# Stick-breaking heads: one summed tile for the last two key blocks

## The chip, the cores and the metric

The kernel runs on one core of a Trainium2 chip. The metric is the device time of one execution in microseconds. It is taken as the median of several runs; a profile is one further execution, recorded instruction by instruction. TensorE (PE in the profile) multiplies matrices into PSUM, VectorE (DVE) and ScalarE (ACT) do elementwise work, GpSimd (POOL) does a little masking and some transfers, and SyncE (SP) issues most transfers.

## The reference, cut to what matters

The program is one transformer block over 512 tokens of width 1024, in float32: a normalisation with modulation, a wide input projection, sixteen stick-breaking attention heads of width 64, four retention heads, a gated merge, and a feed-forward layer. The change touches only the stick-breaking heads:

```python
def stick_breaking_attention(q, k, v):
    s_len = q.shape[2]
    scale = SB_HEAD_DIM ** -0.5
    outs = []
    for i in range(s_len // BLOCK):
        end = (i + 1) * BLOCK
        qb = q[:, :, i * BLOCK:end]
        kb = k[:, :, :end]
        vb = v[:, :, :end]
        z = jnp.einsum('bhtd,bhsd->bhts', qb, kb).astype(jnp.float32) * scale
        ...
        log_1m_beta = jnp.where(mask, jax.nn.log_sigmoid(-z), 0.0)
        after = lax.cumsum(log_1m_beta, axis=3, reverse=True) - log_1m_beta
        log_a = jax.nn.log_sigmoid(z) + after
        a = jnp.where(mask, jnp.exp(log_a), 0.0)
        outs.append(jnp.einsum('bhts,bhsd->bhtd', a.astype(v.dtype), vb))
    return jnp.concatenate(outs, axis=2)
```

For each query the weight of a key is its own log-sigmoid plus the sum, over all later keys up to the query, of the log-sigmoid of the negated score, which is the negative of softplus(z). So a key's logarithm is z minus the sum of softplus over that key and every later one. With keys in blocks of 128, this sum has a part inside the key's own block, which a triangular matrix makes, and a part from all later blocks, for which a matrix of ones is enough.

## The kernel before, in words

**Layout.** Scores are held with keys on the 128 partitions and queries along the columns. Key block j (0 to 3) is needed by queries from j x 128 on, so block 0 has 512 columns, block 1 has 384, block 2 has 256 and block 3 has 128. The table `GEO` gives for each block its PSUM bank, its first column there, its first query and its width. Block 3 is held 256 wide, from query 256 on, with the mask over the part that it does not need, so that blocks 2 and 3 share one bank of 512 columns. There are three banks a head: bank 0 holds block 0, bank 1 holds block 1, bank 2 holds block 2 in its columns 0 to 255 and block 3 in its columns 256 to 511. Blocks 2 and 3 thus cover the same 256 queries.

**Precision.** TensorE takes its operands rounded, so a number that must keep float32 precision is split into a rounded part and the rest. `split` does that with a copy on ACT (the high part) and a subtraction on DVE (the low part). A product with an exact matrix, such as one of ones, takes two matmuls, one with each part. A product of two split operands takes three (`mm3`).

**One head, `sb_head(h)`.** It takes three banks from the pool of `z` and runs in four stages. First the scores of blocks 3, 2, 1, 0 are multiplied into the banks. Then, for the banks 2, 1, 0 in turn, softplus is computed: a mask with a minimum (line 607, DVE), the negated absolute value by an integer operation (609, DVE), exponential and logarithm (612 and 613, ACT), the sum with max(z, 0) (614, DVE) into a temporary `t`, and its split (616) into a pair from the pool `s`, kept as `sp[bank]`. In the third stage the suffix sums are subtracted from the scores in PSUM, bank after bank: block j gets `negtri` times its own softplus and `negones` times that of each later block; line 622 makes that list of terms and line 626 issues two matmuls for each. When a bank is complete, ACT takes its exponential (630) and it is split again (632). Fourth, the values are multiplied into a single bank `av` (640), ACT copies it out (642), a transfer exchanges the two halves of the partitions (644) and DVE adds them (645) into `o_sb`.

So for the third stage block 3 has one term, block 2 has two, block 1 three and block 0 four.

**Order.** Above the heads, the program is written as a sequence: for two pairs of heads at a time, the query and key projections (`sb_qk`, two products of 24 matmuls each) and some of the sixteen gates (`mix`, 24 matmuls each), then four heads, and so on; after the last heads come the last six gates, the splits of the results, and the output product `ps`. The order on each engine is not the written one. A planner at build time keeps, for each instruction, its place in the sequence as its priority, plays the program through with its own estimates of durations, and gives an engine the earliest written instruction that is ready. Matmuls of a projection or a gate, which are written later, therefore fill holes in which a head's next matmul isn't ready. On the chip each engine works through its queue in the order fixed by the planner and stands when the next instruction isn't ready.

**Buffers.** The temporaries `t` have seven slots for tiles of 128x512, the pairs `s` have eight, the banks `z` three, the banks `ps` four, `av` one; weights pass through three `raw`, four `whi` and four `wlo` tiles. SyncE's queue issues its transfers in one order, so an exchange at line 644 that waits holds the weight loads (line 202) behind it.

Of the kernel before, what the change touches and what calls it, by code (L numbers as in the profile page):

```python
# [12 lines left out]
F32R = mybir.dt.float32r  # L13
# [6 lines left out]
P = 128  # L20
D = 1024
S = 512
# [71 lines left out]
BUFS = dict(raw=3, araw=2, whi=4, wlo=4, h=8, q=8, v=4, s=8, qp=2, o=8, t=7, ps=4, z=3, av=1, sm=12)  # L94
# [16 lines left out]
GEO = ((0, 0, 0, 512), (1, 0, 128, 384), (2, 0, 256, 256), (2, 256, 256, 256))  # L111
# [4 lines left out]
def kernel(  # L116
# [9 lines left out]
    nc = tc.nc  # L126
# [3 lines left out]
    apool = ctx.enter_context(tc.tile_pool(name="apool", bufs=1))  # L130
# [5 lines left out]
    def nm(s):  # L136
        uid[0] += 1
        return f"{s}_{uid[0]}"
# [4 lines left out]
    def psa():  # L143
        return pspool.tile([P, S], F32, tag="av", bufs=BUFS["av"], name=nm("av"))

    def psz():
        return pspool.tile([P, S], F32, tag="z", bufs=BUFS["z"], name=nm("z"))

    def pair(tag):
        return apool.tile([P, 2, S], F32R, tag=tag, bufs=BUFS[tag], name=nm(tag))  # L150

    def tmp():
        return apool.tile([P, S], F32, tag="t", bufs=BUFS["t"], name=nm("t"))
# [7 lines left out]
    def f(ap):  # L161
        return ap.bitcast(F32)
# [32 lines left out]
    negtri = cpool.tile([P, P], F32R, name="negtri")  # L195
    negones = cpool.tile([P, P], F32R, name="negones")
# [8 lines left out]
    def split(dst_hi, dst_lo, src, scale=1.0, eng=None):  # L205

        nc.scalar.activation(dst_hi, src, AF.Copy, scale=scale)  # L207
        if isinstance(scale, float) and scale == 1.0:
            return (eng or nc.vector).tensor_sub(dst_lo, src, f(dst_hi))  # L209
        return nc.vector.scalar_tensor_tensor(  # L210
            dst_lo, src, scale, f(dst_hi), op0=ALU.mult, op1=ALU.subtract
        )
# [15 lines left out]
    def mm(o, lhs, rhs, start, stop):  # L228
        return nc.tensor.matmul(o, lhs, rhs, start=start, stop=stop, skip_group_check=True).ins  # L229
# [208 lines left out]
    with tc.manual_schedule(engines={nc.vector.engine, nc.scalar.engine, nc.tensor.engine}):  # L438

        nc.scalar.preload_act_table_set("natural_log_exp_and_others")  # L440
        c = sm[:, SM_C : SM_C + KT]
# [68 lines left out]
        for kt in range(KT):  # L510
# [12 lines left out]
            z = kt == KT - 1  # L523
# [70 lines left out]
    def sb_head(h):  # L594
        q, k, vt = sbq[h], sbk[h], sbv[h // 4]
        z = [psz(), psz(), psz()]
        for j in (3, 2, 1, 0):
            bank, c, t0, w = GEO[j]
            for i in range(2):
                head_pe[h] = mm(z[bank][:, c : c + w], k[:, j * P : (j + 1) * P], q[:, i, t0:S],  # L600
                                i == 0 and j != 2, i == 1)
        sp = {}
        for bank in (2, 1, 0):
            w = BANKW[bank]
            zb = z[bank][:, :w]
            m = S if bank == 2 else P
            nc.vector.tensor_tensor(zb[:, :m], zb[:, :m], maskc[:, :m], op=ALU.min)
            t = tmp()[:, :w]
            nc.vector.tensor_scalar(
                t.bitcast(I32), zb.bitcast(I32), -(2**31), None, op0=ALU.bitwise_or  # L610
            )
            nc.scalar.activation(t, t, AF.Exp)
            nc.scalar.activation(t, t, AF.Ln, bias=1.0)
            nc.vector.scalar_tensor_tensor(t, zb, 0.0, t, op0=ALU.max, op1=ALU.add)
            hl = pair("s")
            split(hl[:, 0, :w], hl[:, 1, :w], t)
            sp[bank] = hl
        avs = {}
        for bank in (2, 1, 0):
            for j in (3, 2) if bank == 2 else (bank,):  # L620
                _, c, t0, w = GEO[j]
                terms = [(negtri, j, t0)] + [(negones, jj, GEO[jj][2]) for jj in range(j + 1, 4)]
                for lhs, jj, tt in terms:
                    bj, cj, tj, wj = GEO[jj]
                    for i in range(2):
                        mm(z[bank][:, c + tt - t0 : c + w], lhs, sp[bj][:, i, cj : cj + wj],
                           False, False)
            w = BANKW[bank]
            t = tmp()[:, :w]
            nc.scalar.activation(t, z[bank][:, :w], AF.Exp)  # L630
            hl = pair("s")
            split(hl[:, 0, :w], hl[:, 1, :w], t)
            avs[bank] = hl
        o = psa()
        r, hf = (h % 4) // 2, h % 2
        for j in (3, 2, 1, 0):
            bank, c, t0, w = GEO[j]
            v = vt[j // 2][:, j % 2, r * 256 + hf * P : r * 256 + hf * P + P]
            for i in range(2):
                mm(o[:, t0:S], v, avs[bank][:, i, c : c + w], j == 3 and i == 0, j == 0 and i == 1)  # L640
        u, u2 = tmp(), tmp()
        nc.scalar.activation(u, o, AF.Copy)
        own, oth = (slice(0, HD), slice(HD, P)) if hf == 0 else (slice(HD, P), slice(0, HD))
        nc.sync.dma_start(u2[own], u[oth])
        nc.vector.tensor_add(o_sb[h // 2][own], u[own], u2[own])
# [3 lines left out]
    def sb_pair(p):  # L649
        o_sb[p] = otile()  # L650
        sb_head(2 * p)
        sb_head(2 * p + 1)
# [445 lines left out]
    for g, n in enumerate((2, 2, 4, 6)):  # L1098
        if g > 1:
            sb_v(g)  # L1100
        for p in (2 * g, 2 * g + 1):
            o_sb[p] = otile()
            for h in (2 * p, 2 * p + 1):
                with tc.issue_after(act_table.ins):
                    sb_head(h)
        if g < 3:
            sb_qk(2 * g + 2)
            mix(n // 2)
            sb_qk(2 * g + 3)
            mix(n - n // 2)  # L1110
        else:
            mix(n)
# [6 lines left out]
    for d in range(8):  # L1119
        o = ps()  # L1120
        gemm(o, weight(("ps", d)), acts)
        r, t = tmp(), tmp()
# [248 lines left out]
    for d in range(4):  # L1371
# [9 lines left out]
        with tc.issue_after(last_sq.ins), tc.issue_after(res.ins):  # L1381
# [3 lines left out]
            elif d == 1:  # L1385
                prepare(0, 2, "qq")
                t0 = sums_of[0]
# [340 lines left out]
```

## Time and profile before

| | |
|---|---|
| median of 3 runs | 1173.94 us (1172.72 to 1175.59) |
| span of the profiled execution | 1173.1 us |
| granted TensorE clock, mean | 0.998 |
| first mask of a head (line 607) | 492.6 us |
| first mask of the last bank of the last head | 714.0 us |
| HBM traffic over the span | 141 GB/s |

The profile's span is one execution's time from its first to its last instruction. A view that groups instructions names them by line, engine, operation and tile (`z<-s,negones` writes a `z` bank from an `s` tile and `negones`), then gives the count, the busy time and the mean of one in ns. Most matmuls stand at line 229, the helper that issues them, so they are told apart by tiles and shapes. A row of the timeline gives the start, the length and the merged count of like instructions that follow each other. Matmuls overlap, so the length of one is more than the distance from its start to the next one's. PEld is the load of the stationary operand.

### The profile page before, as it was taken

To read this page: it belongs to the slowest core of one execution; us is meant where nothing else is said; L and a number is where in the kernel's file an instruction comes from. 1 tells how busy PE (TensorE), PEld (TensorE's weight loads), DVE (VectorE), ACT (ScalarE), POOL (GpSimd) and SP (SyncE) were. 2 spreads that over 40 slices of the span, in tenths; PEclk is the share of its full clock that TensorE was granted. 3 is DMA by queue.
4 is the path that set the end of the run, shared out by engine and by line. 5 is a ranking of instruction groups with operands and counts; after the bars stand their busy time and mean duration, and the time that the engine had idled before them with its cause. 6 is when DMAs were issued, how large, how long until landed. Compare 5 with 4: busy or idle time off the path is not lost.

```text
span 1173.1 us, 16899 instructions
## 1 busy us (share of the span) xinstructions
PE 1156.8 (99%) x6476; PEld 1010.9 (86%) x6476; DVE 873.2 (74%) x1342; ACT 611.9 (52%) x928; POOL 50.1 (4%) x84
## 2 busy tenths in 40 slices
PE   8999999999999999999999999999999999999996
PEld 7898888888878888888888888879999999999996
DVE  7979966775764867478888688775998776777556
ACT  5444543343333444478778688354954444454433
POOL 0000000020002010000000000000100000000000
PEclk9999999999999999999999999999999999999999
DMA  9723536493566565846565545873545663565232
GB/s 358 256 68 113 185 103 208 154 260 115 161 201 176 181 159 185 232 123 180 153 173 133 153 126 179 283 235 103 113 136 179 184 161 116 148 186 152 86 89 72
DMA packets 64017, 192.88 MB, mean 164 GB/s; under 512 B 7744, under 2 KB 9920, under 8 KB 63936
## 3 DMA queue, kind: packets, MB, share of 16 engines
q1 hardware_dynamic: 56624, 172.92, 46.3%
q0 software_dynamic: 6768, 18.35, 8.8%
q8 instruction: 51, 0.84, 0.3%
q10 hardware_dynamic: 544, 0.52, 0.1%
q14 instruction: 30, 0.25, 0.1%
HBM read 146.15 MB, written 18.87 MB: 141 GB/s over the span
## 4 chain that ended last, share of the span: by engine, by line
PE 89%; DVE 4%; DMA 3%; ACT 2%; issue 1%; SPq 0%; DVEq 0%; ACTq 0%
PE ps L229 65%; PE z L229 21%; PE av L229 3%; DMA raw<-wp 2%; DMA araw<-wada 1%; DVE sraw L387 1%; ACT whi L207 1%; DVE wlo L209 1%; DMA o<-xT 0%; ACT s L207 0%; DVE wlo L418 0%; DVE t L425 0%; DVE araw L257 0%; DMA gspill<-g 0%; DVE t L476 0%
## 5 line engine op out<-in xcount | busy, mean ns | idle before, releaser
L229 PE MATMUL ps<-h,whi 128*128 128x512 f32 (+1 forms) x1410 | 416.9, 377 | 1.6 <-DVE h L209 0.8
L229 PEld LDWEIGHTS ps<-h,whi 128*128 128x128 f32 x1410 | 256.2, 188 | 47.7 <-ACT h L431 1.8
L229 PE MATMUL ps<-h,wlo 128*128 128x512 f32 (+1 forms) x705 | 262.1, 376 | 0.0
L207 ACT ACTIVATE whi<-raw 128x1024 fp32r<-128x1024 f32 (+1 forms) x122 | 127.4, 1044 | 192.3 <-PE ps L229 144.8
L209 DVE TENSOR_TENSOR wlo<-raw,whi 128x1024 fp32r<-128x1024 f32 (+1 forms) x122 | 146.6, 1204 | 61.9 <-ACT whi L207 60.8
L229 PEld LDWEIGHTS ps<-h,wlo 128*128 128x128 f32 x705 | 132.8, 188 | 23.2
L229 PE MATMUL ps<-s,whi 128*128 128x512 f32 x480 | 148.5, 390 | 0.7 <-DVE v L209 0.6
L229 PE MATMUL z<-q,whi 128*128 128x256 f32 x504 | 106.8, 283 | 0.0
L229 PEld LDWEIGHTS ps<-s,whi 128*128 128x128 f32 x480 | 89.2, 188 | 19.3 <-DVE v L209 1.0
L229 PE MATMUL ps<-s,wlo 128*128 128x512 f32 x240 | 93.4, 389 | 0.0
L207 ACT ACTIVATE s<-t 128x512 fp32r<-128x512 f32 (+1 forms) x134 | 74.4, 586 | 34.8 <-DVE t L789 21.4
L209 DVE TENSOR_TENSOR s<-t,s 128x512 fp32r<-128x512 f32 (+1 forms) x134 | 81.3, 637 | 9.6 <-ACT s L207 9.3
L229 PEld LDWEIGHTS z<-q,whi 128*128 128x128 f32 x504 | 84.9, 192 | 1.5
L1166 DVE SCALAR_TENSOR_TENSOR o<-ps,mod,o 128x512 f32<-128x512 f32 (+1 forms) x63 | 42.4, 680 | 32.6 <-PE ps L229 32.6
L229 PEld LDWEIGHTS ps<-s,wlo 128*128 128x128 f32 x240 | 45.1, 188 | 9.5
L877 ACT ACTIVATE whi<-s 128x1024 fp32r<-128x1024 f32 x33 | 34.9, 1056 | 33.6 <-PE ps L229 19.0
L229 PE MATMUL ps<-whi,h 128*128 128x512 f32 (+1 forms) x192 | 52.4, 354 | 0.0
L881 DVE TENSOR_TENSOR wlo<-s,whi 128x1024 fp32r<-128x1024 f32 x32 | 39.1, 1222 | 16.3 <-ACT whi L877 15.9
L229 PE MATMUL ps<-q,whi 128*128 128x256 f32 (+1 forms) x224 | 49.3, 313 | 0.0
L229 PE MATMUL z<-qp,whi 128*128 128x256 f32 x168 | 47.2, 283 | 0.0
L229 PE MATMUL z<-q,wlo 128*128 128x256 f32 x168 | 46.4, 283 | 0.0
L257 DVE SCALAR_TENSOR_TENSOR araw<-araw,cact 128x1024 f32<-128x1024 f32 x32 | 38.4, 1221 | 10.0 <-DMA araw<-wada 9.8
(311 smaller groups left out, 2063.1 us busy)
## 6 DMA issues: line engine op xcount, KB each, us to landing
raw<-wp SPq DMA_DIRECT2D x151, 512.0 KB, 4.0
araw<-wada SPq DMA_DIRECT2D x32, 512.0 KB, 4.5
araw<-wp SPq DMA_DIRECT2D x26, 512.0 KB, 4.6
sraw<-wada SPq DMA_DIRECT2D x16, 512.0 KB, 7.8
q<-qp SPq DMA_DIRECT2D x32, 256.0 KB, 3.7
s<-wp SPq DMA_DIRECT2D x12, 512.0 KB, 5.2
spill<-o POOLq DMA_DIRECT2D x24, 256.0 KB, 7.2
o<-xT SPq DMA_DIRECT2D x16, 256.0 KB, 3.7
```

Of the source, the lines that this page charges most:

```text
L207: nc.scalar.activation(dst_hi, src, AF.Copy, scale=scale)
L209: return (eng or nc.vector).tensor_sub(dst_lo, src, f(dst_hi))
L229: return nc.tensor.matmul(o, lhs, rhs, start=start, stop=stop, skip_group_check=True).ins
L257: nc.vector.scalar_tensor_tensor(raw, raw, 1.0, cact, op0=ALU.mult, op1=ALU.mult, accum_out=col)
L387: nc.vector.scalar_tensor_tensor(raw, raw, 1.0, cact, op0=ALU.mult, op1=ALU.mult, accum_out=col)
L877: nc.scalar.activation(hi, t, AF.Copy)
L881: nc.vector.tensor_sub(lo, t, f(hi))
L1166: return nc.vector.scalar_tensor_tensor(x1[d][:, hv], o[:, hv], mod[:, gcol + d : gcol + d + 1], x1[d][:, hv], op0=ALU.mult, op1=ALU.add,)
```

## The change

After the softplus of all three banks, the softplus of blocks 2 and 3, which lie side by side in bank 2's temporary and cover the same 256 queries, is added in place, and the sum is split into a tile `late` from the pool `t` (one tile holds both parts, 256 columns each). Blocks 1 and 0 then multiply `negones` with `late` once where they multiplied it with block 2 and with block 3. Block 0 keeps its separate term for block 1, and block 2 its term for block 3.

```diff
--- before.py
+++ after.py
@@ -615,16 +615,25 @@
             hl = pair("s")
             split(hl[:, 0, :w], hl[:, 1, :w], t)
             sp[bank] = hl
+            if bank == 2:
+                t2 = t
+        late = apool.tile([P, S], F32R, tag="t", bufs=BUFS["t"], name=nm("late")).rearrange("p (a b) -> p a b", a=2)
+        nc.vector.tensor_add(t2[:, 0:256], t2[:, 0:256], t2[:, 256:512])
+        split(late[:, 0, 0:256], late[:, 1, 0:256], t2[:, 0:256])
         avs = {}
         for bank in (2, 1, 0):
             for j in (3, 2) if bank == 2 else (bank,):
                 _, c, t0, w = GEO[j]
-                terms = [(negtri, j, t0)] + [(negones, jj, GEO[jj][2]) for jj in range(j + 1, 4)]
-                for lhs, jj, tt in terms:
-                    bj, cj, tj, wj = GEO[jj]
+                terms = [(negtri, t0, sp[bank][:, :, c : c + w])]
+                if j == 2:
+                    terms.append((negones, 256, sp[2][:, :, 256:512]))
+                elif j < 2:
+                    if j == 0:
+                        terms.append((negones, P, sp[1][:, :, 0:384]))
+                    terms.append((negones, 256, late[:, :, 0:256]))
+                for lhs, tt, x in terms:
                     for i in range(2):
-                        mm(z[bank][:, c + tt - t0 : c + w], lhs, sp[bj][:, i, cj : cj + wj],
-                           False, False)
+                        mm(z[bank][:, c + tt - t0 : c + w], lhs, x[:, i, :], False, False)
             w = BANKW[bank]
             t = tmp()[:, :w]
             nc.scalar.activation(t, z[bank][:, :w], AF.Exp)
```

## The prediction

> **What bounds the kernel now.** I read the page's busy table first, then the chain of waits by engine, then busy time by stretches around the stage that is edited.
>
> ```profile
> span 1173.1 us, 16899 instructions
> ...
> PE 1156.8 (99%) x6476; PEld 1010.9 (86%) x6476; DVE 873.2 (74%) x1342; ACT 611.9 (52%) x928; POOL 50.1 (4%) x84
> ...
> PE 89%; DVE 4%; DMA 3%; ACT 2%; issue 1%; SPq 0%; DVEq 0%; ACTq 0%
> ```
>
> ```profile
> 490.00:550.00 60.00, 59.95 (x308) 50.27 (x307) 47.55 (x81) 46.14 (x83) 0.00 (x0) 1.00 0.58 153
> 550.00:610.00 60.00, 60.00 (x306) 49.80 (x305) 49.74 (x84) 45.99 (x86) 0.00 (x0) 1.00 0.59 167
> 610.00:670.00 60.00, 60.00 (x305) 50.20 (x304) 47.88 (x77) 45.72 (x84) 0.00 (x0) 1.00 0.54 145
> 670.00:730.00 60.00, 60.00 (x309) 50.77 (x308) 49.55 (x82) 52.66 (x97) 0.00 (x0) 1.00 0.47 147
> 730.00:790.00 60.00, 58.81 (x258) 48.16 (x257) 43.81 (x60) 25.36 (x31) 1.73 (x2) 1.00 0.80 260
> ```
>
> The columns of the second fence are the stretch, then busy us of PE, PEld, DVE, ACT and POOL, the granted clock, the DMA share and GB/s. The sixteen heads run from 492 to 731 us, and there TensorE is never idle, at full clock. The heads alone could not do that: the projections of later pairs and the gates fill the holes of the heads' dependency chain.
>
> ```profile
> L229 PE MATMUL ps<-h,whi 128*128 128x512 f32 x422 | 135.5, 391 | 0.0
> ...
> L229 PE MATMUL z<-s,negones 128*128 128x256 f32 x160 | 26.8, 281 | 0.0
> ...
> L229 PE MATMUL z<-s,negones 128*128 128x384 f32 x32 | 8.3, 340 | 0.0
> ```
>
> These are groups of 490 to 730 us: group, count, busy us, mean ns of one. The first is the fill; with one `wlo` matmul to two `whi`, it is 633 matmuls. So the stage is a **queue of matmuls with fill to spare**: what leaves TensorE there leaves the time, as long as nothing new makes TensorE stand.
>
> The waits it has now, in the same stretch (who waited for whom: us, times, longest):
>
> ```profile
> PEld av L229 <- DVE s L209: 2.8, 10, 0.3
> PEld z L229 <- ACT s L207: 2.7, 11, 0.4
> PEld z L229 <- ACT t L630: 2.4, 9, 0.4
> ```
>
> That is 7.9 us in 30 waits, 0.26 us each and no longer than 0.4, for sixteen heads. A hand-off from DVE or ACT to TensorE is thus mostly covered by fill, and where it is not it costs a quarter of a microsecond.
>
> **Removed.** Per head the `negones` matmuls are twelve: two for block 2, four of 256 columns for block 1, and two of 384 and four of 256 for block 0 (192 in all, the 160 and 32 above). After the change blocks 1 and 0 take one product pair with the summed tile where they took two, so four matmuls of 128x256 go per head, **64 in all**. Their price is the distance between starts, since their ends overlap:
>
> ```profile
> 600.85 0.64 PE L229 MATMUL z<-s,negones 128*128 128x256 f32 x4
> ...
> 718.56 0.62 PE L229 MATMUL ps<-h,whi 128*128 128x512 f32 x2
> ```
>
> Four of 256 columns take 0.64 us, the last one 0.28 (its mean above), so a step is (0.64 - 0.28) / 3 = 0.120 us. For 512 columns it is 0.62 - 0.39 = 0.23, about twice that, so a step goes with the columns and not with the weight load. 64 x 0.120 = **7.7 us**. The other end is the busy share of the group, 26.8 / 160 = 0.168 us, which has some tails of lone matmuls in it: 10.7 us. I take 7.7, since these stand in runs.
>
> The Trainium skill, TensorE: Matmul & The Clock Gate, section on the back-to-back issue gap, gives N/2.4 + 2.5 ns for the gap of a lone matmul, 109 ns for 256 columns; by that the 64 would be an estimated 7.0 us. The trace has 120 ns, so the sum goes by that.
>
> **Added.** Per head an add of 128x256 on DVE, a copy of 128x256 on ACT and a subtraction of 128x256 on DVE. No DMA is added and none moves past another. The same forms stand elsewhere in this trace:
>
> ```profile
> L1407 DVE TENSOR_TENSOR t<-t,t 128x256 f32<-128x256 f32 x16 | 6.8, 422 | 3.9 <-ACT t L1403 2.7 <-ACT t L1576 1.2
> L207 ACT ACTIVATE s<-t 128x256 fp32r<-128x256 f32 x8 | 2.8, 404 | 0.4 <-DVE t L1040 0.4
> L209 DVE TENSOR_TENSOR s<-t,s 128x256 fp32r<-128x256 f32 x8 | 2.9, 418 | 0.0
> ```
>
> So 0.84 us of DVE and 0.40 us of ACT a head, 13.4 and 6.5 us in all. DVE was busy for 194.7 of the 240 us (the four rows added), ACT for 190.5; they go to 208 and 197 of about 235. Both still have room, so as work they cost nothing. The room is what hides them: without it, the two rows that grow would be a bound themselves.
>
> **Moved: the wait.** This is the term that can go either way. Block 1 could run when its own and bank 2's parts were split; now its last pair waits for the sum, whose three steps are issued behind all three banks. One head, in time:
>
> ```profile
> 607.56 1.74 DVE L609 TENSOR_SCALAR t<-z 128x512 int32<-128x512 int32 x3
> ...
> 612.03 0.68 DVE L209 TENSOR_TENSOR s<-t,s 128x512 fp32r<-128x512 f32 x1
> ...
> 612.63 0.68 DVE L614 SCALAR_TENSOR_TENSOR t<-z,t 128x512 f32<-128x512 f32 x1
> ...
> 614.30 1.22 DVE L209 TENSOR_TENSOR wlo<-raw,whi 128x1024 fp32r<-128x1024 f32 x1
> ...
> 614.75 0.64 PE L229 MATMUL z<-s,negones 128*128 128x256 f32 x4
> ...
> 615.42 0.49 ACT L630 ACTIVATE t<-z 128x384 f32<-128x384 f32 x1 [0.59 <-PE z L229]
> 615.43 0.68 DVE L209 TENSOR_TENSOR s<-t,s 128x512 fp32r<-128x512 f32 x1
> ...
> 616.47 1.16 DVE L209 TENSOR_TENSOR s<-t,s 128x512 fp32r<-128x512 f32 x2 [0.35 <-ACT s L207]
> ...
> 617.09 1.00 PE L229 MATMUL z<-s,negones 128*128 128x384 f32 x6
> ...
> 618.12 0.60 ACT L630 ACTIVATE t<-z 128x512 f32<-128x512 f32 x1 [1.28 <-PE z L229]
> ...
> 620.41 1.75 DVE L609 TENSOR_SCALAR t<-z 128x512 int32<-128x512 int32 x3
> ```
>
> Bank 2 is split at 612.7 and bank 0 at 616.1. If the three steps follow that, the sum is there at 616.1 + 0.42 + 0.40 + 0.42 = 617.3; if the two subtractions of 616.47 stand ahead of the last step, at 617.6 + 0.42 = 618.0. Two pairs of 0.24 us then end at 617.8 to 618.5. Block 1's exponential so starts some 2 to 3 us later than its 615.4, but block 0's, which ends the head, at most 0.4 us later than its 618.1, and its own 0.6 us behind block 1's 0.5 on ACT makes that up to 0.9. Behind the waiting weight load on TensorE's queue stand fill matmuls, and for their banks the gates on DVE and ACT wait. But the order is the planner's: a term that it expects late is put behind fill, as it does with bank 0 today (its six wait from 615.4 to 617.1 while TensorE is busy). I charge one extra wait of 0.26 us in every second head, 8 x 0.26 = **2.1 us**; the ends are 0 and all three steps bare, 16 x 1.24 = 19.9 us.
>
> What is late next: the next head's banks 1 and 0 and the exchange of halves behind the head, which holds the load queue:
>
> ```profile
> SPq L644 <- ACT t L642: 42.4, 15, 6.0
> ```
>
> It already stands 42.4 us for `u` in 490 to 800 us, 2.8 a time, without TensorE standing; 0.9 more a head at most is a third of that, and I charge nothing for it; it would come back as loads that are as much later, 16 x 0.9 = 14.4 us at the worst, inside the end already named. And heads are not back to back; the mask of a head's last bank and of the next head's first, across the last change of group, start at
>
> ```profile
> 646.04 0.30 DVE L607 TENSOR_TENSOR z<-z,table 128x128 f32<-128x128 f32 x1
> ...
> 672.22 0.89 DVE L607 TENSOR_TENSOR z<-z,table 128x512 f32<-128x512 f32 x2
> ```
>
> 26 us there, against the 12.8 from one head's `L609` to the next in the sequence above: some 13 us of slack before head 12, which is more than 11 x 0.9 = 9.9.
>
> **Buffers.** Nine `t` tiles a head where there were eight, on seven slots, and bank 2's is held until the add. I cost this at nothing: the sum is last read by bank 0's terms, at about 618.5, before the next head takes its three at 620.4. Without those 1.9 us the next head would start as much later as the sum, at most the 1.24 above. In return bank 2's `s` tile is free after block 2.
>
> **Sum.** -7.7 + 2.1 = -5.6. From the span, 1173.1 - 5.6 = 1167.5; the median of the runs, 1173.94, lies 0.8 above this execution's span, which I keep: **1168.3 us**. The stretch behind the heads loses TensorE 1.2 of 60 us to loads (fifth row of the stretches); its loads start as tiles of the heads' stage come free, so it moves along.
>
> **Rivals.**
>
> The heads' chain takes the place of the queue in the last four heads, behind which no further head waits as fill:
>
> ```profile
> 731.59 0.62 PE L229 MATMUL ps<-q,whi 128*128 128x512 f32 x2
> ...
> 731.98 0.69 DVE L209 TENSOR_TENSOR s<-o,s 128x512 fp32r<-128x512 f32 x1 [0.70 <-ACT s L207]
> ...
> 732.72 0.39 PE L229 MATMUL ps<-s,whi 128*128 128x512 f32 x1
> ```
>
> The first output product meets the last head's result just in time. If each of the four is late by the whole 1.24, 5.0 us are given back: 1168.3 + 5.0 = **1173.3**. Against it: at 731.59 the second product is already under way as fill, and its 21 matmuls that don't need that head are 4.8 us.
>
> TensorE has room that its busy share hides: weight loads are 86% of the span, so 14% of the steps might be idle and the removed matmuls come out of that. Then **1173.9**, unchanged. Against it: a load takes 188 ns
>
> ```profile
> L229 PEld LDWEIGHTS ps<-h,whi 128*128 128x128 f32 x1410 | 256.2, 188 | 47.7 <-ACT h L431 1.8
> ```
>
> and the steps of 0.120 us are shorter than that, so loads overlap, while the step doubles with the columns. The Trainium skill, Perfetto Trace Analysis, section on identifying the most-contended engine, says that matmul busy time is a poor measure and weight-load busy a better one; the starts in this trace speak for the columns as the limit.
>
> **Slower:** TensorE stands at the first product with the sum, in each head, because in the run DVE reaches the two added steps later than the planner thought (a `wlo` subtraction of 1.22 us is put in front, as at 614.30). It decides from 7.7 / 16 = 0.48 us of standing a head. With the three steps bare: 1173.9 - 7.7 + 19.9 = **1186.1**. For it: DVE goes from 81% to 88%. Against it: no wait of a weight load is over 0.4 us today.
>
> That the change does not do what it says I leave out: the loop of terms fixes the count.
>
> **How the numbers follow.** Forecast 0.62; the last four heads 0.16; room on TensorE 0.05; slower 0.17. A difference under 0.3%, 3.5 us, can't be told from none. Faster is thus 0.62, the same 0.21, slower 0.17. The forecast's own range is 1163.2 (10.7 removed, no wait) to 1170.4. The range of 8 in 10 runs from 1163 to 1178: it takes in the cases of no change and the near part of the slower one, and leaves out the bare steps.
>
> **What would show it.** 64 `z<-s,negones` matmuls and 64 with the new tile instead of 192; 32 new DVE and 16 new ACT instructions of 0.42 and 0.40 us; TensorE still at 60 of 60 in the four stretches, with the last head's `L645` some 5 us earlier; waits of weight loads for the new tile of about 2 us in total. It is wrong if those waits exceed 4 us, if TensorE shows idle time between 490 and 730 us, or if the heads end earlier but the span does not follow.

## The result and the profile after

| | before | changed |
|---|---|---|
| median of 4 runs each, same chip | 1173.55 us (1172.72 to 1175.59) | 1165.28 us (1164.15 to 1166.38) |
| ratio, 95% interval | | 0.9928 [0.9914, 0.9942] |
| span of the profiled execution | 1173.1 us | 1164.4 us |

The changed kernel is 8.3 us faster, 0.7%; the forecast was 5.6 us, and the time lies in its range. From line 628 on, lines of the changed kernel are 9 higher than before.

The page of the changed kernel, span, busy time and chain of waits:

```profile
span 1164.4 us, 16817 instructions
...
PE 1149.4 (99%) x6412; PEld 1003.9 (86%) x6412; DVE 882.9 (76%) x1374; ACT 616.8 (53%) x944; POOL 50.0 (4%) x84
...
PE 90%; DVE 4%; DMA 3%; ACT 2%; issue 1%; SPq 0%; DVEq 0%; ACTq 0%
```

There are 64 matmuls fewer, 32 DVE and 16 ACT instructions more. PE's busy time fell by 7.4 us and the span by 8.7. The groups of the changed kernel between 490 and 730 us (busy us, mean ns, idle before):

```profile
L229 PE MATMUL z<-late,negones 128*128 128x256 f32 x64 | 15.3, 289 | 0.0
...
L209 DVE TENSOR_TENSOR late<-t,late 128x256 fp32r<-128x256 f32 x16 | 6.7, 417 | 0.2 <-ACT late L207 0.2
L621 DVE TENSOR_TENSOR t<-t 128x256 f32<-128x256 f32 x16 | 6.6, 415 | 0.0
L207 ACT ACTIVATE late<-t 128x256 fp32r<-128x256 f32 x16 | 6.5, 407 | 0.6 <-DVE t L621 0.5
L229 PE MATMUL z<-s,negones 128*128 128x256 f32 x32 | 6.4, 282 | 0.0
```

With the 32 of 384 columns this is 64 and 64, as the forecast had it, at nearly the durations that it took from other stages (422 and 418 ns on DVE, 404 on ACT). The stretches of the changed kernel (busy us of PE, PEld, DVE, ACT and POOL, granted clock, DMA share, GB/s):

```profile
490.00:550.00 60.00, 60.00 (x303) 50.26 (x302) 52.44 (x92) 47.21 (x87) 0.00 (x0) 1.00 0.62 168
550.00:610.00 60.00, 60.00 (x300) 50.08 (x299) 51.32 (x91) 46.99 (x87) 0.00 (x0) 1.00 0.62 169
610.00:670.00 60.00, 60.00 (x301) 50.37 (x300) 53.59 (x93) 52.27 (x99) 0.00 (x0) 1.00 0.56 148
670.00:730.00 60.00, 59.71 (x295) 48.92 (x294) 49.60 (x84) 50.34 (x93) 0.00 (x0) 1.00 0.51 163
730.00:790.00 60.00, 59.51 (x282) 49.72 (x281) 47.72 (x64) 28.84 (x34) 2.58 (x3) 1.00 0.83 263
```

TensorE is still full while the heads run, but for 0.29 us in the fourth stretch. Its longest groups of waits there, 485 to 728 us, and the one for the new tile (us, times, longest):

```profile
PEld z L229 <- ACT s L207: 3.3, 15, 0.4
PEld av L229 <- ACT s L207: 1.6, 7, 0.4
...
PEld z L229 <- ACT late L207: 0.9, 3, 0.4
```

So the new wait is met three times in sixteen heads. One head of the changed kernel in time shows why:

```profile
615.54 0.61 ACT L207 ACTIVATE s<-t 128x512 fp32r<-128x512 f32 x1
615.71 0.41 DVE L621 TENSOR_TENSOR t<-t 128x256 f32<-128x256 f32 x1
...
616.16 0.42 ACT L207 ACTIVATE late<-t 128x256 fp32r<-128x256 f32 x1
...
616.64 0.68 DVE L209 TENSOR_TENSOR s<-t,s 128x512 fp32r<-128x512 f32 x1
...
617.24 0.41 DVE L209 TENSOR_TENSOR late<-t,late 128x256 fp32r<-128x256 f32 x1
...
617.48 0.28 PE L229 MATMUL z<-late,negones 128*128 128x256 f32 x1
...
618.65 0.40 PE L229 MATMUL z<-late,negones 128*128 128x256 f32 x2
618.68 1.01 ACT L639 ACTIVATE t<-z 128x384 f32<-128x384 f32 x2 [0.95 <-PE z L229]
```

The add at 615.71 runs while ACT copies bank 0, and slips in ahead of bank 0's own low part at 616.64. The sum is complete at 617.65, some 0.3 us behind that low part (617.32), and its last use is at 618.65. That is the common case: by the ends in the trace it is 0.3 us in ten of the sixteen heads, and over 2 us in three. Over the sixteen heads, from the first `L609` of a head to the end of its exponentials, block 1's comes 1.5 us later than before (10.78 us, before 9.27) and block 0's, which ends the head, 0.1 us (11.66, before 11.55); these four are means worked out from the starts and ends of the trace.

Where the gain appears is less plain. The last head's exchange is added (`o`) and the last gate (`g`) is made, in the kernel before, at the last time of each row (count, durations in ns, first to last start):

```profile
L645 DVE TENSOR_TENSOR o<-t,t x16: 673/686/692, 512.2 to 730.6; 64x512 f32<-64x512 f32 x16
```

```profile
L827 DVE TENSOR_SCALAR g<-ps,sm x16: 740/750/751, 475.6 to 727.0; 128x512 f32<-128x512 f32 x16
```

and in the changed kernel:

```profile
L654 DVE TENSOR_TENSOR o<-t,t x16: 671/686/690, 511.6 to 727.7; 64x512 f32<-64x512 f32 x16
```

```profile
L836 DVE TENSOR_SCALAR g<-ps,sm x16: 741/750/751, 475.8 to 717.6; 128x512 f32<-128x512 f32 x16
```

The heads end only 2.9 us earlier, the last gate 9.4 us earlier. The matmuls that were freed let the fill run ahead, while a head has become a little longer: 17.8 us from its first `L609` to its `o`, where it was 17.3 (means of sixteen). The rest of the gain is had behind the heads, where less fill is left over: from the last head's row to the end of the span it is 442.5 us before (1173.1 - 730.6) and 436.7 after (1164.4 - 727.7). The distance from the last gate to the last head grew from 3.6 to 10.1 us; it matters in the experiments.

### The profile page after: what moved, and what is told of

Its sections match the earlier page's. It is cut to its first block, busy times and chain, and to the rows that moved or that the text cites. A ratio compares the mean times of both kernels' runs of the same rounds, so it can differ in the third digit from the quotient of the medians.

```text
span 1164.4 us, 16817 instructions
## 1 busy us (share of the span) xinstructions
PE 1149.4 (99%) x6412; PEld 1003.9 (86%) x6412; DVE 882.9 (76%) x1374; ACT 616.8 (53%) x944; POOL 50.0 (4%) x84
## 4 chain that ended last, share of the span: by engine, by line
PE 90%; DVE 4%; DMA 3%; ACT 2%; issue 1%; SPq 0%; DVEq 0%; ACTq 0%
PE ps L229 66%; PE z L229 21%; PE av L229 3%; DMA raw<-wp 2%; DVE sraw L387 1%; DVE wlo L209 1%; ACT whi L207 1%; DMA t<-t 1%; DVE araw L257 0%; DMA araw<-wada 0%; DVE wlo L418 0%; ACT s L207 0%; DVE t L425 0%; DVE t L1135 0%; DVE fin L1620 0%
## 5 line engine op out<-in xcount | busy, mean ns | idle before, releaser
L229 PE MATMUL z<-q,q 128*128 128x256 f32 (+2 forms) x224 | 45.9, 326 | 0.0
```

## The experiments

Each is compared with the kernel before on its own chip. "Against the change" is the difference of the two distances to that kernel.

**Parts of the change.** The first builds the sum and does not use it:

```diff
-                    terms.append((negones, 256, late[:, :, 0:256]))
+                    terms.append((negones, 256, sp[2][:, :, 0:256]))
+                    terms.append((negones, 256, sp[2][:, :, 256:512]))
```

> Makes the sum and splits it, but multiplies blocks 2 and 3 separately as the kernel before does (the output is complete, the summed tile is not read). Queue theory (TensorE's count of matmuls sets the time): DVE and ACT have room, so 1173.5 us, within 2 us of the kernel before. Rival (the gain came from a luckier order or other buffers): near 1165 to 1169. Rival (the elementwise work costs): 1175 or more.

Measured: 1173.46 us, ratio 0.9995 [0.9987, 1.0004]. Three instructions a head cost nothing that can be told.

The second keeps the wait and the old number of matmuls: half the sum, multiplied twice.

```diff
-        split(late[:, 0, 0:256], late[:, 1, 0:256], t2[:, 0:256])
+        split(late[:, 0, 0:256], late[:, 1, 0:256], t2[:, 0:256], 0.5)
...
-                    terms.append((negones, 256, late[:, :, 0:256]))
+                    terms += [(negones, 256, late[:, :, 0:256])] * 2
```

> Splits half of the sum and multiplies it twice, so that blocks 1 and 0 wait for the summed tile as after the change, while the count of matmuls is that of before. Queue theory: the 64 matmuls of 0.120 us come back, 1165.3 + 7.7 = 1173 us, within 2 us of the kernel before; the wait is worth the difference to the run that makes the sum and does not use it, 0 to 2 us. Rival (the wait is a real cost that the removed matmuls outweighed): 1175 to 1180.

Measured: 1173.6 us, ratio 0.9995 [0.9986, 1.0004]. The wait costs 0.1 us against the first experiment, which is nothing within intervals of 1 us each way. From here to the change only the 64 matmuls go, and the time falls by 8.0 us, 0.125 us a matmul (by the two intervals, some 2 us either way). In this profile the last head and the last gate stand at

```profile
L654 DVE TENSOR_TENSOR o<-t,t x16: 674/686/690, 511.4 to 735.1; 64x512 f32<-64x512 f32 x16
```

```profile
L836 DVE TENSOR_SCALAR g<-ps,sm x16: 742/751/751, 476.5 to 724.4; 128x512 f32<-128x512 f32 x16
```

Compared with this kernel, the change brings the heads' end forward by 7.4 us and the last gate by 6.8: with the wait in both, the heads do go with TensorE's queue. The wait by itself is the step from the first experiment, in whose profile the last head stands at 730.6 and the last gate at 721.6. It moves them back by 4.5 and 2.8 us, and block 0 is done 0.4 us later in a head (11.72 us from the first `L609`, there 11.29, means of sixteen), while the medians agree. The fill takes the places that the heads leave, and so the wait is paid in order, not in time. These places are of one execution of each kernel, that of the first experiment being its fastest (1170.82 us, median 1173.46).

**Without fill.** Both kernels again, with the projections and gates of a group of heads held until that group's last head has issued its value products:

```diff
-                mm(o[:, t0:S], v, avs[bank][:, i, c : c + w], j == 3 and i == 0, j == 0 and i == 1)
+                last_av[0] = mm(o[:, t0:S], v, avs[bank][:, i, c : c + w], j == 3 and i == 0, j == 0 and i == 1)
...
-        if g < 3:
...
+        with tc.issue_after(last_av[0]):
+            if g < 3:
...
```

> The kernel before, with the projections and gates that fill the heads' holes queued behind each group of four heads on TensorE. The holes are open: 14 us a head less some 5.4 us of its own matmuls, so 80 to 140 us more than before, 1255 to 1315 us. It is the base for the next run.

> The same without fill for the changed kernel. If cover is what makes the wait free, the wait shows here: 16 heads by up to 0.9 us, so 0 to 14 us slower than the run without fill of the kernel before. Rival (the wait costs nothing in itself, since four matmuls fewer make it up): 0 to 8 us faster than it.

Measured: 1295.62 us for the kernel before (ratio 1.1037 [1.1021, 1.1054]) and 1287.8 us for the changed one (1.0968 [1.095, 1.0986]), 7.8 us less. The fill is worth 122 us. And without it the sum still gains, as the rival had it and not my theory. One head of the kernel before without fill, bank 0's softplus and its exponential:

```profile
611.21 0.68 DVE L614 SCALAR_TENSOR_TENSOR t<-z,t 128x512 f32<-128x512 f32 x1
...
614.89 1.70 PE L229 MATMUL z<-s,negones 128*128 128x384 f32 x6
616.62 0.60 ACT L630 ACTIVATE t<-z 128x512 f32<-128x512 f32 x1 [1.30 <-PE z L229]
```

and of the changed kernel without fill:

```profile
610.32 0.69 DVE L614 SCALAR_TENSOR_TENSOR t<-z,t 128x512 f32<-128x512 f32 x1
...
611.38 0.42 DVE L621 TENSOR_TENSOR t<-t 128x256 f32<-128x256 f32 x1
611.84 0.42 ACT L207 ACTIVATE late<-t 128x256 fp32r<-128x256 f32 x1 [0.17 <-DVE t L621]
...
614.87 0.60 ACT L639 ACTIVATE t<-z 128x512 f32<-128x512 f32 x1 [0.58 <-PE z L229]
```

From the one to the other it is 5.4 us before and 4.55 us after. The wait is not longer than what the matmuls gave back, so it is not the fill alone that hides it: the sum is there in time for block 0's terms. That the gain is again close to 8 us does not make the wait nothing here. TensorE is slower without fill, 0.213 us between the starts of two such matmuls where it is 0.118 with fill (medians of the kernel before), so the 64 would be worth up to 13.6 us, and the wait can have cost the rest.

**A later sum.** If the sum had slack, a delay should cost little. Two GpSimd passes that leave the sum as it is:

```diff
         nc.vector.tensor_add(t2[:, 0:256], t2[:, 0:256], t2[:, 256:512])
+        for _ in range(2):
+            nc.gpsimd.affine_select(
+                t2[:, 0:256], t2[:, 0:256], pattern=[[1, 256]], compare_op=ALU.is_ge, fill=0.0, base=P,
+                channel_multiplier=-1,
+            )
```

and the same with eight passes.

> Two passes of GpSimd over the sum that change nothing stand between the add and the copy, some 0.8 us plus hand-offs, on an engine that is idle there; the planner knows of them. Queue theory: fill covers it, within 2 us of the changed kernel's 1165.3. Rival (the wait for the sum is just covered and any more of it shows): 16 x 1 us, 1175 to 1181.

> Eight such passes, 3.2 us and hand-offs per head. Queue theory: still mostly covered before the last group of heads, where the fill runs out: some 0 to 4 x 4 us on top, 1165 to 1181. Rival (each head's delay shows in full): 16 x 4 = 64 us, 1229.

Measured: 1176.23 us with two (ratio 1.0024 [1.0013, 1.0035]), 10.8 us over the change, and 1242.93 with eight (1.059 [1.0575, 1.0606]). My expectation of at most 2 us for the two passes was a miss, its rival's 1175 to 1181 holds; with eight the time is above both, the rival's 1229 too. The passes and the waits for the new tile in the kernel with two:

```profile
L623 POOL TENSOR_SCALAR_AFFINE_SELECT t<-t x32: 398/641/1311, 499.5 to 729.2; 128x256 f32<-128x256 f32 x32
```

```profile
PEld z L229 <- ACT late L207: 12.2, 14, 1.9
```

A delay of 1.28 us a head (two of 0.641, the median) is met in 14 heads by TensorE standing for 12.2 us in all, about the whole loss. This loss is a matter of order: the product was put at a place where the sum wasn't there yet, and what could have filled the hole was queued behind it.

Is it the delay, or that it was not foreseen? The next kernel delays the sum with two ACT copies of it onto itself:

```diff
         nc.vector.tensor_add(t2[:, 0:256], t2[:, 0:256], t2[:, 256:512])
+        for _ in range(2):
+            nc.scalar.activation(t2[:, 0:256], t2[:, 0:256], AF.Copy)
```

> The changed kernel with two ACT copies of the sum onto itself ahead of its split, about 0.4 us each by ACT's rows of this shape, so the sum is there about 0.8 to 1.0 us later, as against 1.1 us with the two GpSimd passes, which cost 10.9 us. Theory (the planner knows the length of an ACT copy and puts the product behind other work; the GpSimd passes it took for shorter): 1166 to 1169. Rival (any delay of the sum shows in full, 16 heads by 0.5 to 0.9 us): 1173 to 1180.

Measured: 1171.79 us, ratio 0.9987 [0.9977, 0.9996], 6.9 us over the change: between the two expectations. Two stretches, the wait for the tile, and the last gate and head:

```profile
670.00:730.00 60.00, 58.35 (x287) 47.98 (x287) 50.67 (x90) 55.60 (x109) 0.00 (x0) 1.00 0.44 144
730.00:790.00 60.00, 57.30 (x247) 45.39 (x246) 46.20 (x64) 27.74 (x34) 1.73 (x2) 1.00 0.79 253
```

```profile
PEld z L229 <- ACT late L207: 1.3, 5, 0.3
```

```profile
L838 DVE TENSOR_SCALAR g<-ps,sm x16: 739/750/751, 475.6 to 712.3; 128x512 f32<-128x512 f32 x16
```

```profile
L656 DVE TENSOR_TENSOR o<-t,t x16: 673/686/692, 511.5 to 734.0; 64x512 f32<-64x512 f32 x16
```

Here TensorE hardly stands for the sum: 1.3 us. The delay of 0.82 us (two copies of 408 ns) was covered in place, by fill drawn forward. So the last gate is made 5.3 us earlier than in the change and the last head ends 6.3 us later; in the 21.7 us between them too little is ready, and 4.35 of 120 us are idle, where the change had 0.78. Counted by starts of matmuls, in excess of the median distance for each width, the two stretches lose 9.1 us and those of the change 3.1, so most of the 6.9 us is lost there. Not all of it is a lack of matmuls: two of the pieces, 0.77 us at 741.2 and 0.74 at 753.1, are the output product waiting for the low part of its weights.

So what differs from the GpSimd passes is the place of the loss. The price is not shown to differ: 10.8 us for 16 x 1.28 and 6.9 us for 16 x 0.82 are both 0.53 us for each us of delay. Whether it was foreseeing that moved the loss stays open.

The last kernel leaves the two copies out of the last two heads:

```diff
+        for _ in range(2 if h < 14 else 0):
+            nc.scalar.activation(t2[:, 0:256], t2[:, 0:256], AF.Copy)
```

> The changed kernel with the two extra ACT copies of the sum in the first fourteen heads alone, not in the last two. In all sixteen heads they cost 6.3 us against the change, and the trace showed no standing between 690 and 720 us and 6.4 us between 720 and 750 us, behind the last gate. Theory (a delay that the planner knows is hidden by fill as long as there is some, and shows behind the last fill only): with the last two heads as in the change, 1165 to 1167.5. Rival (the fourteen use up the fill, so that the last two stand even without a delay of their own, or the extra 11.5 us of ACT cost as work): 1169 to 1171.8.

Measured: 1172.14 us, ratio 0.9987 [0.9978, 0.9996]: as much as with all sixteen, though a share of fourteen sixteenths, 6.0 us, could not be told from it. My theory that only the heads behind the last fill pay was wrong in this form; the rival holds (0.3 us above its range, inside the interval).

```profile
670.00:730.00 60.00, 58.01 (x289) 48.06 (x288) 50.69 (x89) 54.23 (x105) 0.00 (x0) 1.00 0.45 147
730.00:790.00 60.00, 56.97 (x244) 45.10 (x244) 45.97 (x63) 27.37 (x34) 1.73 (x2) 1.00 0.77 253
```

```profile
L838 DVE TENSOR_SCALAR g<-ps,sm x16: 739/751/751, 476.2 to 712.7; 128x512 f32<-128x512 f32 x16
```

```profile
L656 DVE TENSOR_TENSOR o<-t,t x16: 674/688/691, 512.1 to 734.2; 64x512 f32<-64x512 f32 x16
```

```profile
724.31 0.80 PE L229 MATMUL z<-s,negtri 128*128 128x384 f32 x4 [1.33 <-ACT s L207]
```

The last gate is as early, at 712.7, and the idle time as large, 5.02 of 120 us, with nothing delayed there; the last row, of the timeline, is the longest single piece of it between 715 and 740 us, a head's own split with nothing left to put in. If it is fill that is missing, the debt was run up by the earlier heads. That ACT's extra 11.5 us (28 copies of 0.41) cost as work too is not excluded by this run: two further pieces, 1.18 us at 741.8 and at 754.1, are again the output product waiting for its weights.

**An earlier sum.** The three steps right behind bank 2's softplus should make the wait shorter still:

```diff
             if bank == 2:
                 t2 = t
-        late = apool.tile([P, S], F32R, tag="t", bufs=BUFS["t"], name=nm("late")).rearrange("p (a b) -> p a b", a=2)
-        nc.vector.tensor_add(t2[:, 0:256], t2[:, 0:256], t2[:, 256:512])
-        split(late[:, 0, 0:256], late[:, 1, 0:256], t2[:, 0:256])
+                late = apool.tile([P, S], F32R, tag="t", bufs=BUFS["t"], name=nm("late")).rearrange("p (a b) -> p a b", a=2)
+                nc.vector.tensor_add(t2[:, 0:256], t2[:, 0:256], t2[:, 256:512])
+                split(late[:, 0, 0:256], late[:, 1, 0:256], t2[:, 0:256])
```

> The sum is written right behind bank 2's softplus, ahead of banks 1 and 0. Queue theory: the wait is covered in either place, so within 1.5 us of the changed kernel's 1165.3. Rival (block 1 and 0 standing for the sum cost time that the prediction charged with 2.1 us): 1163. Rival (the place matters the other way, since the sum now delays the softplus of banks 1 and 0): 1167 or more.

Measured: 1215.58 us, ratio 1.0361 [1.0347, 1.0375], 50 us over the change. The last rival had the direction, and that the sum delays the softplus of banks 1 and 0; nothing had the size. One head on DVE:

```profile
599.23 0.30 DVE L607 TENSOR_TENSOR z<-z,table 128x128 f32<-128x128 f32 x1 [0.49 <-PE z L229]
...
600.26 0.29 DVE L607 TENSOR_TENSOR z<-z,table 128x128 f32<-128x128 f32 x1
600.46 0.68 DVE L609 TENSOR_SCALAR t<-z 128x512 int32<-128x512 int32 x1
...
606.48 0.55 DVE L609 TENSOR_SCALAR t<-z 128x384 int32<-128x384 int32 x1
...
607.38 0.68 DVE L609 TENSOR_SCALAR t<-z 128x512 int32<-128x512 int32 x1
```

Banks 1 and 0 are masked at 599.5 and 600.6, but their `L609`, which writes a new temporary, runs only at 606.48 and 607.38, around the time when the sum's pair is first written. In the kernel before the three follow each other (`x3`) in most heads: the third starts 1.1 us behind the first in 13 of 16 heads, in the changed kernel in 14. Here it is 5.5 to 9.7 us in the sixteen heads. The pair was a tile of the pool `t` too, taken ahead of the temporaries of banks 1 and 0. If tiles of one pool are handed out in the written order, those two had to stand until the pair was taken. This can be tried by taking the pair from the pool `s`, with the sum in either place; the edit is the same in both:

```diff
-        late = apool.tile([P, S], F32R, tag="t", bufs=BUFS["t"], name=nm("late")).rearrange("p (a b) -> p a b", a=2)
+        late = pair("s")
```

> The changed kernel, with the sum's pair taken from the eight tiles of tag s (the split softplus and weights) and not from the seven of tag t. Theory: neither ring is short here, the time stays that of the change, 1165.5 us within 1.5. Rival: seven pairs of eight then live within one head, so the next head's first split waits for a pair; the extra standing of TensorE in the eight pairs of heads would make it 1167 to 1180.

> The early sum again (right behind bank 2's softplus), which cost 50 us when its pair was a tile of tag t, now with its pair in tag s. Theory of the order of tiles: in tag t the pair was handed out ahead of the temporaries of banks 1 and 0, so their softplus stood behind it; in tag s it stands ahead of their split pairs alone, which come later anyway, so most of the 50 us goes: 1164 to 1172. Rival (the early place itself costs, by two ACT copies and adds put ahead of the softplus of banks 1 and 0): the time stays near 1215, above 1200 in any case.

Measured: 1166.6 us in the place of the change (ratio 0.9942 [0.9927, 0.9957]), 1.7 us over it with intervals that overlap, and 1178.11 us in the early place (1.0036 [1.0025, 1.0048]). So 37 of the 50 us came from the pool that the pair was in, and the stand of banks 1 and 0 is gone with it, in 15 of 16 heads, as the order of tiles says (how the planner hands them out was not looked into). A head in the early place with the pair in `s`:

```profile
600.31 1.74 DVE L609 TENSOR_SCALAR t<-z 128x512 int32<-128x512 int32 x3
```

The second expectation's 1164 to 1172 was still missed, by 6 us. That rest stays open. The heads are longer than in the change (18.4 us from a head's first `L609` to its `o` against 17.8, means of sixteen), but with the pair in `s` in the later place they are 18.2 at 1166.6 us. As with the ACT copies, idle time shows late, 6.38 of 120 us:

```profile
670.00:730.00 60.00, 56.91 (x284) 46.74 (x283) 51.52 (x89) 51.73 (x99) 0.00 (x0) 1.00 0.48 154
730.00:790.00 60.00, 56.71 (x237) 44.61 (x238) 44.70 (x63) 25.51 (x35) 0.86 (x1) 0.97 0.67 223
```

**One sum more.** Block 0's two terms can be one, if bank 1's softplus is added too; that saves 32 further matmuls.

```diff
+        upto1 = pair("s")
+        nc.vector.tensor_add(t1[:, 128:384], t1[:, 128:384], t2[:, 0:256])
+        split(upto1[:, 0, 0:384], upto1[:, 1, 0:384], t1[:, 0:384])
...
-                    if j == 0:
-                        terms.append((negones, P, sp[1][:, :, 0:384]))
-                    terms.append((negones, 256, late[:, :, 0:256]))
+                    terms.append((negones, P, upto1[:, :, 0:384]) if j == 0 else (negones, 256, late[:, :, 0:256]))
```

> Goes one step further: the sum of blocks 2 and 3 is added to block 1's softplus in a second step, and block 0 multiplies that one tile of 384 columns, so two more matmuls of 256 columns go per head, for one more DVE add of 256, a copy and a subtraction of 384 columns. Queue theory: 32 x 0.120 = 3.8 us less, 1161.5. Rival (DVE, which goes from 205 to 220 of 237 us in the heads, or the longer chain becomes the bound): 1165 to 1175.

Measured: 1183.71 us, ratio 1.0087 [1.0073, 1.0101], 18 us over the change, and above the 1161.5 of the theory and the 1165 to 1175 of the rival. Its last gate and head:

```profile
L839 DVE TENSOR_SCALAR g<-ps,sm x16: 732/750/751, 475.8 to 703.8; 128x512 f32<-128x512 f32 x16
```

```profile
L657 DVE TENSOR_TENSOR o<-t,t x16: 672/686/690, 511.0 to 746.5; 64x512 f32<-64x512 f32 x16
```

Again the gate is earlier and the last head later, with 42.7 us between them. How much of that is the longer chain and how much the further pair that it takes from `s` was not separated. The distance from the last gate to the last head, read from the same two rows of each kernel, orders by their time the kernels that multiply with the sum, fewer matmuls and no GpSimd pass. The last column is the time behind the last head, the span of the profile less that row's last start:

| kernel | distance, us | time over the kernel before, us | behind the last head, us |
|---|---|---|---|
| changed | 10.1 | -8.3 | 436.7 |
| pair in `s` | 15.8 | -6.6 | 435.9 |
| two ACT copies, fourteen heads | 21.5 | -1.5 | 437.1 |
| two ACT copies | 21.7 | -1.4 | 436.4 |
| pair in `s`, early | 25.4 | +4.9 | 437.3 |
| one sum more (96 matmuls fewer, not 64) | 42.7 | +9.8 | 435.9 |
| early | 81.9 | +41.7 | 436.6 |

What is left behind the last head is within 1.4 us the same in all of them, so their times differ by how late the last head ends. With the two GpSimd passes it is 435.0; the kernel before still had more to do there, 442.5.

The kernel with two GpSimd passes is not in the order of the distances, since it stands at the product itself: 12.0 us and +2.5.

No run beat the changed kernel.

## Why the prediction was right, point by point

- **The bound.** TensorE's queue with fill to spare: right. Work added on DVE and ACT cost nothing (0.4 us under the kernel before, inside its interval), 64 matmuls taken out gave 8.0 us. Idle time between 490 and 730 us was named as a sign of being wrong; it is 0.29 us, before 0.05.
- **Removed, 7.7 us.** Right in mechanism and size: 8.0 us by the second experiment, 0.125 us a matmul where 0.120 was taken from the starts, which the runs can't tell apart.
- **The wait, 2.1 us.** This is the term that was mis-sized: "I charge one extra wait of 0.26 us in every second head". It measured 0.1 us of the total, within some 1.5 us, and the waits for the tile in the trace are 3 and not 8. (Its list of today's waits left out two groups, 1.4 us in 5 waits; the mean of 0.26 us hardly changes.) The times in the working were good: the sum was forecast for 617.3 to 618.0 and came at 617.65, block 0 was to be at most 0.4 to 0.9 us later and was 0.1, block 1 was to be 2 to 3 and was 1.5. What they imply, a sum that is there when the head's end needs it or shortly behind, should have been priced at nothing in the total: the heads wait for it, 4.5 us at the last one, but TensorE has fill to do. The difference of 8.3 to 5.6 is this term and the 0.3 us of the one above, within what the runs can tell.
- **The hold over by fill.** "A term that it expects late is put behind fill" fits the ACT copies (1.3 us of standing), and it is not free: they cost 6.9 us, most of it late in the heads and behind them. It failed for the GpSimd passes (12.2 us of standing). That the planner takes a GpSimd pass for shorter than it is was not measured, so foreseen or not is an argument and not a finding.
- **The last head some 5 us earlier.** Wrong: 2.9. The step that failed is not that the heads go with TensorE's queue: without the 64 matmuls they end 7.4 us earlier, against the same kernel with the wait. It is the one price for the wait in both places. The wait holds the heads back by 4.5 us at the last one and the total by 0.1, and what the heads don't gain, the later work does.
- **Buffers at nothing.** Held in the place of the change: another pool for the pair, 1.7 us the other way with overlapping intervals. In another written place the same pool cost 37 us, which the working did not look at.
- **The rival of the last four heads.** In the changed kernel it costs little, 0.78 us of idle time in 120, but that kernel stands at its edge: the time behind the last head, 436.7 us, is already that of the kernels which run into it. As a mechanism it is right: it is what the ACT copies and the further sum run into, and 0.82 us a head is enough for 6.9 us.
- **Room on TensorE.** Refuted: the removed matmuls gave all of their distance of starts. Weight loads are 86% busy before and after; the 14% that this leaves was no room. The Trainium skill, Perfetto Trace Analysis, section on identifying the most-contended engine, has TensorE's headroom judged by that share and by the share of peak FLOPs; here the starts of the matmuls tell it, and the share of weight loads does not.
- **The slower rival.** Its mechanism exists and its threshold was about right. It was to decide from 0.48 us of standing a head; with the two GpSimd passes the loss was 10.8 / 16 = 0.68 us a head, and that kernel is slower than before by 2.5 us. In the changed kernel the standing is 0.9 / 16 = 0.06.

## What to carry to other kernels

Where one engine's queue is full and later work fills its holes, taking instructions out of it gains their distance of starts, and an added dependency costs the total nothing if its operand comes in the shade of one that is waited for anyway; so compare the two arrival times before charging a wait. A dependency that comes later was not hidden by fill for nothing in these runs: the fill seems to be borrowed from the end of the stage. The distance between the last fill and the last of the dependent chain shows how much is still left, and once none is, the time goes with the end of that chain. Before moving a small step in the written order, look at which pool its result is taken from and what takes from it next.

## What the runs showed that I had not expected

- A tile taken from one pool instead of another was worth 37 us with the same instructions, in one written place, and 1.7 us the other way, within overlapping intervals, in another.
- Two delays showed in different places: 1.28 us a head on GpSimd as TensorE standing at the product in 14 of 16 heads, 0.82 us a head on ACT hardly at the product (1.3 us) but as idle time behind the last gate. For their length they cost the same.
- Without fill the granted clock is lower too. This is the kernel before with its fill held back, 490 to 670 us (PE, PEld, DVE, ACT and POOL busy us, clock, DMA share, GB/s):

```profile
490.00:670.00 180.00, 137.91 (x593) 115.61 (x591) 100.72 (x165) 97.61 (x168) 0.00 (x0) 0.86 0.40 110
```

TensorE is busy for 77% of that stretch at a clock of 0.86, and a `negones` matmul of 256 columns takes 396 ns there on average, with fill 281. So the holes of the heads cost more than their own length.
